# Feed-forward of a hybrid decoder layer: both products done one after the other, the second as seven products of block sums whose weight sums are made in DRAM

## The chip, the cores and the metric

The kernel runs on one core of one Trainium2 chip. The metric is device time in microseconds (us) of one launch. TensorE is called PE below, its weight loads PEld, VectorE DVE, ScalarE ACT, GpSimd POOL; SyncE is called SP and here only issues DMAs.

## The reference, cut to what matters

One layer on 512 tokens of width 2048, all in float32. A mixer (spatial gating, short convolution, gated DeltaNet) is followed by this feed-forward, a gated per-layer embedding and a last norm:

```python
h = h + concat([ya, yb, yc]) @ w_o                       # 2048 x 2048
hn = rmsnorm(h, norm_ffn)
h = h + square(relu(hn @ w_ff1)) @ w_ff2                 # 2048 -> 8192 -> 2048
hn = rmsnorm(h, norm_ple)
h = h + (p_i @ w_ple_proj) * sigmoid(hn @ w_ple_gate)
return rmsnorm(h, norm_final)
```

## The kernel before

Every float32 operand of a large product is split into a high part (a cast to fp32r, on ACT) and a low part (operand minus high part, on DVE). A product is then three matmuls, high x high, high x low and low x high (`mm3`, or the three matmul lines of `up_group`). Weights are never kept: `wload` takes a piece from DRAM into a ring `wraw` of 2816 columns (DMA on SP's queue), casts it into the ring `wh` (line 178) and subtracts into the ring `wl` (line 179). `wload` runs at a raised priority, `ahead[0]` = 200 instructions ahead of its place. Within an engine the order of instructions is fixed when the program is built, by a list scheduler; on the chip each engine runs its stream in that order.

The stages in order: input norm and first columns of `w_in`; eight DeltaNet heads (pieces of 512 columns, 16 pieces a head, the recurrence of each head mixed in by `tick`, with round trips through DRAM on SP's queue and small operations on POOL); four short convolutions; `w_o` in two halves; the feed-forward; the embedding gate and the output.

The feed-forward's first product (`up_group`) is already done as seven products instead of eight. A group `g` makes 256 hidden features for 512 tokens. For each of the 8 pairs of 128-row blocks of the input width, a 128x512 piece of `w_ff1` (four 128x128 blocks) is loaded, `pair_combos` (lines 887 to 889, DVE) adds three combinations, the whole 128x896 piece is split, and 7 x 3 matmuls of 256 columns follow. The matching combinations of the activations were made once by `fast_tiles`. At the end of a group some additions on DVE (lines 918 to 923) put the seven results together, then relu, square and a split leave the hidden features in SBUF, in one of three slots of `hidden`.

The second product (`down`) is plain. Of 16 chunks of 512 hidden features, each is multiplied with four 512-column pieces of `w_ff2` (`wload` of 128x1024), 48 matmuls of 512 columns each, and added into the residual rows `hs` in SBUF by DVE (`accumulate`, line 780). The loop at the end of the quoted text interleaves the two: one `up_group` pair of blocks, then half a `down`, so that both products run through the whole feed-forward. The up product takes the four PSUM banks `pd`, the down product the four banks `pg`. There are 32 groups, 5,376 matmuls of 256 columns, and 16 x 4 pieces, 3,072 matmuls of 512 columns.

Of the kernel before, what the change touches and what calls it, by code (L numbers as in the profile page):

```python
# [10 lines left out]
F32 = mybir.dt.float32  # L11
# [8 lines left out]
P = 128  # L20
S = 512
# [34 lines left out]
def hybrid_block(ctx: ExitStack, tc: tile.TileContext, x, p, norm_mix, w_in, sg_ln_g, sg_ln_b, sg_w,  # L56
# [102 lines left out]
    def wload(shape, parts, dst=None, combine=None):  # L159
        n = int(np.prod(shape))  # L160
        at = place(n)

        def view(t):
            t = t[:, at:at + n]
            if len(shape) == 1:
                return t
            if len(shape) == 2:
                return t.rearrange("q (a b) -> q a b", a=shape[0])
            return t.rearrange("q (a b c) -> q a b c", a=shape[0], b=shape[1])
        rv = view(ring[0])  # L170
        if dst is None:
            dst = view(ring[1]), view(ring[2])
        with tc.high_priority(offset=ahead[0]):
            for sel, src in parts:
                nc.sync.dma_start(sel(rv), src)
            if combine:
                combine(rv)
            nc.scalar.copy(dst[0], rv)  # L178
            nc.vector.tensor_tensor(dst[1], rv, dst[0].bitcast(F32), ALU.subtract)  # L179
        return dst  # L180

    def seg_parts(wdram, segs, k0, kc):
# [318 lines left out]
    if True:  # L501
# [180 lines left out]

        done = [False] * H
        gd = None
        for h in range(H):
            c = {"h": h}
            ps = [pd.tile([P, S], F32, name="d") for _ in range(2)]
            if h == 0:
                drain()
                later(sgu())  # L690
            feature_major(col_blocks(w_in, [QKV0 + 1024 + h * P, QKV0 + h * P]), 2, KD, KC2, ps)
            if h == 0:
                drain()
# [12 lines left out]
            gate_z(c, ps[1])  # L706
# [141 lines left out]
    for part in (1, 0):  # L848
        for c in range(4):
            ps, pool, nm = banks()  # L850
            token_major(w_o[part * 1024:(part + 1) * 1024], [(c * 512, 512)], lambda k: mix(8 * part + k)[0],
                        lambda k: mix(8 * part + k)[1], 8, ps, KC3)
            if part and c == 0:
                drain()
            if part:
                for tt in range(NT):
                    accumulate(tt, c, ps[tt])
                if c == 3:
                    xb = [r2b.tile([P, 16, HS], F32R, name="r2") for _ in range(2)]
# [22 lines left out]
            yield  # L882

    ss2 = res.tile([P, NT, 4], F32, name="ss2")
    def pair_combos(v):
        b = v.rearrange("q (a b) -> q a b", b=P)
        nc.vector.tensor_tensor(b[:, 4:6], b[:, 0:4:3], b[:, 1:2].broadcast_to([P, 2, P]), ALU.subtract)  # L887
        nc.vector.tensor_tensor(b[:, 1], b[:, 3], b[:, 4], ALU.add)
        nc.vector.tensor_tensor(b[:, 6], b[:, 2], b[:, 1], ALU.subtract)

    def up_group(g, pool, nm):
        ba, bb, bc_, bd = (pool.tile([P, 2, HS], F32, name=nm) for _ in range(4))

        def src(j):
            return w_ff1[2 * j * P:(2 * j + 2) * P, g * 256:(g + 1) * 256].rearrange("(a q) c -> q a c", q=P)
        for i, j in enumerate(PAIRS):
            wh, wl = wload((7 * P,), [(lambda v: v[:, :4 * P].rearrange("q (a c) -> q a c", a=2), src(j))],
                           combine=pair_combos)
            k = 2 * j
            e = list(zip(*([t[:, q] for t in z for q in range(t.shape[1])] for z in extra[j])))  # L900
            xs = [(XH[:, k, :HS], XL[:, k, :HS]), (XH[:, k + 1, :HS], XL[:, k + 1, :HS]), e[2],
                  (XH[:, k + 1, HS:], XL[:, k + 1, HS:]), e[0], e[1], (XH[:, k, HS:], XL[:, k, HS:])]
            for m, (slot, dst, half) in enumerate(((0, bc_, 0), (2, ba, 0), (3, bd, 0), (6, ba, 1), (4, bc_, 1),
                                                   (1, bb, 0), (5, bb, 1))):
                ws = slice(slot * P, (slot + 1) * P)
# [24 lines left out]
        yield  # L930

    NCH = DFF // 512
    hidden = [(t[:, o:o + 4].rearrange("q (a b) c -> q a (b c)", a=2), t[:, o + 4:o + 8].rearrange("q (a b) c -> q a (b c)", a=2))
              for t, o in ((hb[0], 0), (hb[0], 8), (hb[1], 0))]

    def up():
        for g in range(2 * NCH):
            yield from up_group(g, *((pg, "g") if g == 1 else (pd, "d")))

    def down(ch, c):  # L940
        ps, pool, nm = banks() if ch == NCH - 1 else ([pg.tile([P, 512], F32, name="g") for _ in range(NT)], pg, "g")
        for half in range(2):
            hh, hl = hidden[(2 * ch + half) % 3]
            k0 = 4 * ch + 2 * half
            wh, wl = wload((2, 512), seg_parts(w_ff2, [(c * 512, 512)], k0, 2))
            for a in range(2):
                for tt in range(NT):
                    ts = slice(tt * P, (tt + 1) * P)
                    mm3(ps[tt], hh[:, a, ts], hl[:, a, ts], wh[:, a], wl[:, a], not half and a == 0, half == 1 and a == 1)
                    tick()  # L950
            if half and ch < NCH - 1:
                for tt in range(NT):
                    accumulate(tt, c, ps[tt], rf)
            yield
        if ch == NCH - 1:
            residual(c, ps, pool, nm, ss2, KD, rf)
# [19 lines left out]
    for c in range(4):
        for _ in down(NCH - 1, c):
            pass
        if c == 1:
            pk = r2b.tile([P, 8, S], F32R, name="r2")  # L980
            pH, pL = pk[:, 0:2], pk[:, 2:4]
            entry = bg.pop()
            later(chain(entry[0], load_p(pd, "d")), entry[1])
# [86 lines left out]
```

## Time and profile before

| what | value |
|---|---|
| median of 3 runs | 2475.78 us (2475.64 to 2476.18) |
| span of the profiled execution | 2472.7 us |
| median less that span | 3.1 us |
| busy: PE, DVE, ACT, POOL | 2453.9, 1534.0, 949.1, 150.7 us |
| granted clock, mean | 0.999 |
| DMA moved | 257.30 MB, 104 GB/s over the span |

The span runs from the first to the last instruction; what is left of a run's time lies before and after it. For the profiled execution no other time than its span is listed. Busy PE counts time from a matmul's start to its modelled end, and matmuls overlap, so the pace of PE is read from the starts of neighbouring matmuls. DMA share is the mean busy share of the core's 16 DMA engines.

### The profile page before, as it was taken

How to read it: one execution, taken by the hardware profiler on the slowest of the kernel's cores; microseconds unless marked ns; L12 is line 12 of the kernel's file. 1: busy time of each engine (PE TensorE's matmuls, PEld its weight loads, DVE VectorE, ACT ScalarE, POOL GpSimd, SP SyncE). 2: the span in 40 equal slices, each digit the busy share in tenths (PEclk: the TensorE clock that was granted, in tenths of full speed). 3: DMA queues.
4: the chain of work that ended last, by engine and by line, in shares of the span. 5: the costliest groups of instructions: out<-in, count | busy, mean ns of one | idle time of the engine just before them, and what ended most of it. 6: DMA issues, size and time to landing. Idle time of an engine off the chain costs nothing.

```text
span 2472.7 us, 36948 instructions
## 1 busy us (share of the span) xinstructions
PE 2453.9 (99%) x14236; PEld 2161.9 (87%) x14236; DVE 1534.0 (62%) x2704; ACT 949.1 (38%) x1587; POOL 150.7 (6%) x325
## 2 busy tenths in 40 slices
PE   9999999999999999999999999999999999999998
PEld 8988888888888888899999999999999999987888
DVE  6754555544553477767676777767676767665334
ACT  5433333333432354333333333333333333345333
POOL 1422222222000000000000000000000000000000
PEclk9999999999999999999999999999999999999999
DMA  6433333332334223333333333333333333332233
GB/s 216 118 92 100 94 95 92 91 89 78 110 110 162 94 69 107 102 101 95 103 100 103 103 103 103 102 99 102 99 94 103 103 103 103 103 109 95 100 102 116
DMA packets 264997, 257.30 MB, mean 104 GB/s; under 512 B 29626, under 2 KB 209651, under 8 KB 263923
## 3 DMA queue, kind: packets, MB, share of 16 engines
q1 hardware_dynamic: 261796, 248.38, 32.8%
q10 hardware_dynamic: 3024, 6.55, 0.8%
q8 instruction: 112, 1.84, 0.3%
q14 instruction: 65, 0.53, 0.1%
HBM read 242.00 MB, written 12.86 MB: 103 GB/s over the span
## 4 chain that ended last, share of the span: by engine, by line
PE 92%; DVE 1%; DMA 1%; ACT 0%; issue 0%; POOL 0%; POOLq 0%; ACTq 0%
PE g L219 12%; PE g L220 12%; PE g L218 12%; PE d L911 8%; PE d L909 8%; PE d L910 8%; PE d L266 6%; PE d L268 6%; PE d L267 6%; PE d L218 2%; PE d L220 2%; PE d L219 2%; PE g L511 1%; PE g L611 1%; DMA wraw<-in_w_ff_dram 1%; PE g L618 1%
## 5 line engine op out<-in xcount | busy, mean ns | idle before, releaser
L178 ACT CAST wh<-wraw 128x896 fp32r<-128x896 f32 (+4 forms) x704 | 577.0, 821 | 1152.6 <-PE g L220 529.9
L179 DVE TENSOR_TENSOR wl<-wraw,wh 128x896 fp32r<-128x896 f32 (+4 forms) x704 | 668.0, 950 | 558.1 <-ACT wh L178 528.1
L218 PE MATMUL g<-wh,r 128*128 128x512 f32 x1128 | 440.6, 391 | 1.3 <-ACT r L224 1.2
L219 PE MATMUL g<-wl,r 128*128 128x512 f32 x1128 | 441.6, 391 | 0.2 <-DVE wl L179 0.2
L220 PE MATMUL g<-wh,r 128*128 128x512 f32 x1128 | 441.3, 392 | 0.0
L266 PE MATMUL d<-XH,wh 128*128 128x512 f32 x704 | 293.5, 417 | 0.0
L911 PE MATMUL d<-XL,wh 128*128 128x256 f32 x992 | 279.7, 282 | 0.7 <-DVE XL L228 0.7
L910 PE MATMUL d<-XH,wl 128*128 128x256 f32 x992 | 278.4, 281 | 0.7 <-DVE wl L179 0.7
L909 PE MATMUL d<-XH,wh 128*128 128x256 f32 x992 | 278.3, 281 | 0.0
L268 PE MATMUL d<-XL,wh 128*128 128x512 f32 x704 | 275.8, 392 | 0.0
L267 PE MATMUL d<-XH,wl 128*128 128x512 f32 x704 | 275.5, 391 | 0.0
L220 PEld LDWEIGHTS g<-wh,r 128*128 128x128 f32 x1128 | 211.7, 188 | 45.1
L218 PEld LDWEIGHTS g<-wh,r 128*128 128x128 f32 x1128 | 211.9, 188 | 43.6 <-ACT r L224 2.2
L219 PEld LDWEIGHTS g<-wl,r 128*128 128x128 f32 x1128 | 211.8, 188 | 42.3 <-DVE wl L179 0.5
L910 PEld LDWEIGHTS d<-XH,wl 128*128 128x128 f32 x992 | 187.2, 189 | 5.7 <-DVE wl L179 0.9
L909 PEld LDWEIGHTS d<-XH,wh 128*128 128x128 f32 x992 | 187.7, 189 | 5.1 <-issue 0.3
L911 PEld LDWEIGHTS d<-XL,wh 128*128 128x128 f32 x992 | 187.3, 189 | 1.1 <-DVE XL L228 1.1
L887 DVE TENSOR_TENSOR wraw<-wraw 128x256 f32<-128x256 f32 x256 | 108.0, 422 | 125.7 <-DMA wraw<-in_w_ff_dram 124.9
L910 PE MATMUL d<-r,wl 128*128 128x256 f32 x651 | 184.1, 283 | 0.0
L909 PE MATMUL d<-r,wh 128*128 128x256 f32 x651 | 183.7, 282 | 0.0
L780 DVE SCALAR_TENSOR_TENSOR h<-g,rf,h 128x512 f32<-128x512 f32 x248 | 178.9, 744 | 2.3 <-PE g L220 2.3
L911 PE MATMUL d<-r,wh 128*128 128x256 f32 x589 | 165.5, 281 | 0.0
(343 smaller groups left out, 3754.4 us busy)
## 6 DMA issues: line engine op xcount, KB each, us to landing
wraw<-in_w_ff_dram SPq DMA_DIRECT2D x256, 256.0 KB, 2.7
wraw<-in_w_ff_dram SPq DMA_DIRECT2D x128, 512.0 KB, 3.7
wraw<-in_w_in_dram SPq DMA_DIRECT2D x352, 128.0 KB, 2.3
wraw<-in_w_o_dram SPq DMA_DIRECT2D x64, 256.0 KB, 2.9
wraw<-in_w_ple_gate_dram SPq DMA_DIRECT2D x64, 256.0 KB, 2.9
h<-in_x_dram ACTq DMA_DIRECT2D x4, 1024.0 KB, 7.9
wraw<-in_w_in_dram SPq DMA_DIRECT2D x16, 196.0 KB, 2.6
x<-in_x_dram SPq DMA_DIRECT2D x3, 1024.0 KB, 7.3
```

The lines of the kernel that those rows point to most:

```text
L178: nc.scalar.copy(dst[0], rv)
L179: nc.vector.tensor_tensor(dst[1], rv, dst[0].bitcast(F32), ALU.subtract)
L218: nc.tensor.matmul(ps, ah, bh, start=start, stop=False)
L219: nc.tensor.matmul(ps, ah, bl, start=False, stop=False)
L220: nc.tensor.matmul(ps, al, bh, start=False, stop=stop)
L266: nc.tensor.matmul(ps, wh[:, a, b], XH[:, k], start=k == 0, stop=False)
L267: nc.tensor.matmul(ps, wl[:, a, b], XH[:, k], start=False, stop=False)
L268: nc.tensor.matmul(ps, wh[:, a, b], XL[:, k], start=False, stop=k == nk - 1)
L780: nc.vector.scalar_tensor_tensor(hc, ps, scale[:, tt:tt + 1], hc, ALU.mult, ALU.add)
L909: nc.tensor.matmul(ps, wh[:, ws], xh, start=i == 0 and m in (0, 1, 2, 5), stop=False)
L910: nc.tensor.matmul(ps, wl[:, ws], xh, start=False, stop=False)
L911: nc.tensor.matmul(ps, wh[:, ws], xl, start=False, stop=stop)
```

## The change

The two products are done one after the other.

- Groups 0 and 1 run as before. Then the residual rows `hs` (4 MB) are stored to DRAM, and their SBUF space becomes buffers for pieces of twice the size: three raw pieces and two each of high and low part, of 128x1792 (two pairs of blocks). Groups 2 to 31 use these (`up_weights`), alternately with the banks `pd` and `pg`.
- At the end of a group the hidden features are not split. Seven 128x256 tiles (four blocks and three sums) are made by three more DVE operations and written to DRAM by POOL's DMA (`hd`, 0.92 MB a group in rows of 1 KB).
- The second product views tokens as two halves, output columns as two halves of 1024, and hidden features as 32 pairs of 128-row blocks. It is done as seven products (`product`), each over the 32 pairs, each with 12 matmuls of 512 columns a pair: 2,688 matmuls. Each of the four tiles in PSUM is added into `hs` and into a scratch array after the product. Three products read `w_ff2` itself, four read sums of its blocks, `qd[0]` to `qd[3]`, 16 MB each, from DRAM. For each pair 128x1024 weights (0.5 MB) are loaded and split, for each four pairs 128x1024 activations.
- The sums `qd` are made by `presum`: 64 DMAs of 1 MB on SP's queue that copy a block from DRAM to DRAM, and 64 DMAs of 1 MB on POOL's queue that add another block onto it. `count`, called at each `wload`, issues one of these 128 steps for every 4 loads, from the first DeltaNet head on, and for every 3 loads from group 2 on (a piece of two pairs counts 2). In each round four copies are followed by four additions to copies of earlier rounds. 32 loads were counted before the first head, so 8 copies are issued there together.
- The residual rows are loaded again (4 MB) before the second product. The transposes for the gate are put behind product 6 and its end.

```diff
+NG = DFF // 256
+NST = NG // 2
+FW = D // 2
...
             nc.vector.tensor_tensor(dst[1], rv, dst[0].bitcast(F32), ALU.subtract)
+        count()
         return dst
...
+    qd = [[dram.tile([P, 2, FW + 16], F32, name=f"q{i}_{st}")[:, :, :FW] for st in range(NST)] for i in range(4)]
+    w2v = w_ff2.rearrange("(st b a q) c -> st a q b c", b=2, a=2, q=P)
+
+    def w2block(st, a, f):
+        return w2v[st, a][:, :, f * FW:(f + 1) * FW]
+
+    def presum():
+        for i in range(NST + 3):
+            if i < NST:
+                for q, a, f in ((0, 0, 0), (2, 1, 1), (3, 1, 0), (1, 1, 1)):
+                    tc.keep_in_program_order(nc.sync.dma_start(qd[q][i], w2block(i, a, f)))
+                    yield
+            for q, lag in ((0, 1), (2, 1), (1, 2), (3, 3)):
+                st = i - lag
+                if 0 <= st < NST:
+                    other = w2block(st, 0, 1) if lag == 1 else qd[0 if q == 1 else 1][st]
+                    tc.keep_in_program_order(nc.gpsimd.dma_start(qd[q][st], other, accum_op=ALU.add))
+                    yield
+
+    sums = presum()
+    pace = [0, 0]
+
+    def count(n=1):
+        pace[0] += n
+        while pace[1] and pace[0] >= pace[1]:
+            pace[0] -= pace[1]
+            next(sums, None)
...
+        pace[1] = 4
         for h in range(H):
...
     def pair_combos(v):
-        b = v.rearrange("q (a b) -> q a b", b=P)
-        nc.vector.tensor_tensor(b[:, 4:6], b[:, 0:4:3], b[:, 1:2].broadcast_to([P, 2, P]), ALU.subtract)
-        nc.vector.tensor_tensor(b[:, 1], b[:, 3], b[:, 4], ALU.add)
-        nc.vector.tensor_tensor(b[:, 6], b[:, 2], b[:, 1], ALU.subtract)
+        b = v.rearrange("q (j a b) -> q j a b", b=P, a=7)
+        n = b.shape[1]
+        for j in range(n):
+            nc.vector.tensor_tensor(b[:, j, 4:6], b[:, j, 0:4:3], b[:, j, 1:2].broadcast_to([P, 2, P]), ALU.subtract)
+        nc.vector.tensor_tensor(b[:, :, 1], b[:, :, 3], b[:, :, 4], ALU.add)
+        nc.vector.tensor_tensor(b[:, :, 6], b[:, :, 2], b[:, :, 1], ALU.subtract)
+
+    wide = []
+
+    def up_weights(g, i):
...
+        rv, wh, wl = (t[n % len(t)] for t in wide)
+        with tc.high_priority(offset=ahead[0]):
+            for j in range(2):
+                nc.sync.dma_start(rv[:, j * 7 * P:j * 7 * P + 4 * P].rearrange("q (a c) -> q a c", a=2), src(i + j))
+            pair_combos(rv)
+            nc.scalar.copy(wh, rv)
+            nc.vector.tensor_tensor(wl, rv, wh.bitcast(F32), ALU.subtract)
+        count(2)
+        return wh, wl
...
-        hh, hl = hidden[g % 3]
-        for o, t in ((0, sa), (1, v)):
-            nc.scalar.activation(t, t, AF.Relu)
-            nc.scalar.activation(t, t, AF.Square)
-            dh, dl = (z[:, o].rearrange("q (a b) -> q a b", a=2) for z in (hh, hl))
-            split(dh, dl, t)
...
+        nc.scalar.activation(s[:, :4], s[:, :4], AF.Relu)
+        nc.scalar.activation(s[:, :4], s[:, :4], AF.Square)
+        nc.vector.tensor_tensor(s[:, 4:6], s[:, 0:4:3], s[:, 2:3].broadcast_to([P, 2, HS]), ALU.subtract)
+        nc.vector.tensor_tensor(s[:, 6], s[:, 0], s[:, 5], ALU.add)
+        nc.vector.tensor_tensor(s[:, 2], s[:, 6], s[:, 1], ALU.subtract)
+        nc.gpsimd.dma_start(hd[g // 4][:, :, g % 4].rearrange("m q c -> q m c"), s)
+
+    up_group(0, pd, "d")
+    up_group(1, pg, "g")
     spot[0] = 0
     drain()
...
+    for tt in range(NT):
+        nc.sync.dma_start(hsd[tt], hs[tt])
+    hctx.close()
+    wp = hctx.enter_context(tc.tile_pool(name="wp", bufs=1))
...
+    pace[1] = 3
+    for g in range(2, NG):
+        up_group(g, *((pd, "d"), (pg, "g"))[g % 2])
+    for _ in sums:
         pass
+    hctx.close()
...
+    for tt in range(NT):
+        nc.sync.dma_start(hs[tt], hsd[tt])
...
+    def product(m, slot, wsrc):
+        pool, nm = ((pd, "d"), (pg, "g"))[m % 2]
+        ps = [[pool.tile([P, 512], F32, name=nm) for _ in range(2)] for _ in range(2)]
+        for kp in range(NG):
+            n = m * NG + kp
+            rv, wh, wl = wslots[n % len(wslots)]
+            with tc.high_priority(offset=ahead[0]):
+                if kp % 4 == 0:
...
+                    nc.sync.dma_start(xr_, hd[kp // 4][slot])
+                    split(xh, xl, xr_)
+                nc.sync.dma_start(rv, wsrc(kp))
+                split(wh, wl, rv)
+            for t in range(2):
+                ts = slice(t * P, (t + 1) * P)
+                for f in range(2):
+                    fs = slice(f * 512, (f + 1) * 512)
+                    mm3(ps[t][f], xh[:, kp % 4, ts], xl[:, kp % 4, ts], wh[:, fs], wl[:, fs], kp == 0, kp == NG - 1)
+                tick()
+        return ps
...
+    ps = product(3, 4, q2(2))
+    for t, f in PAIR4:
+        nc.vector.tensor_tensor(u(t, f), u(t, f), ps[t][f], ALU.add)
+        add(2 + t, f, u(t, f))
+        add(2 + t, 2 + f, ps[t][f], -1)
+        square(2 + t, 2 + f, ps[t][f])
...
```

There are four places `wslots` for the weights of `product`: two in the old rings, two in the space that held activation combinations of the up product (`xr`, `xb`).

## Rows read from the trace of the kernel before

**Rows 1.** The page: busy time by engine; chain that ended last, by engine.

```profile
PE 2453.9 (99%) x14236; PEld 2161.9 (87%) x14236; DVE 1534.0 (62%) x2704; ACT 949.1 (38%) x1587; POOL 150.7 (6%) x325
...
PE 92%; DVE 1%; DMA 1%; ACT 0%; issue 0%; POOL 0%; POOLq 0%; ACTq 0%
```

**Rows 2.** Windows of 62 us (`w_o`, feed-forward): busy, clock, DMA share, GB/s.

```profile
744.00:806.00 62.00, 62.00 (x268) 50.28 (x267) 23.03 (x35) 13.65 (x22) 0.00 (x0) 1.00 0.45 161
...
1488.00:1550.00 62.00, 62.00 (x392) 56.12 (x391) 45.15 (x80) 24.62 (x32) 0.00 (x0) 1.00 0.31 98
```

**Rows 3.** Timeline of PE in the feed-forward; first number the start.

```profile
1499.78 0.39 PE L218 MATMUL g<-wh,r 128*128 128x512 f32 x1
...
1503.64 0.39 PE L220 MATMUL g<-wh,r 128*128 128x512 f32 x1
1503.87 0.28 PE L909 MATMUL d<-XH,wh 128*128 128x256 f32 x1
...
1505.89 0.28 PE L911 MATMUL d<-r,wh 128*128 128x256 f32 x1
```

**Rows 4.** Groups by line and form: count, busy us, mean ns, idle before.

```profile
L179 DVE TENSOR_TENSOR wl<-wraw,wh 128x896 fp32r<-128x896 f32 x256 | 279.0, 1090 | 177.2 <-ACT wh L178 174.5
...
L178 ACT CAST wh<-wraw 128x896 fp32r<-128x896 f32 x256 | 241.2, 943 | 293.0 <-PE d L911 261.1 <-DVE wl L179 13.7 <-DVE wraw L889 9.5
...
L780 DVE SCALAR_TENSOR_TENSOR h<-g,rf,h 128x512 f32<-128x512 f32 x248 | 178.9, 744 | 2.3 <-PE g L220 2.3
...
L179 DVE TENSOR_TENSOR wl<-wraw,wh 128x1024 fp32r<-128x1024 f32 x128 | 156.1, 1220 | 55.5 <-ACT wh L178 55.5
L178 ACT CAST wh<-wraw 128x1024 fp32r<-128x1024 f32 x128 | 134.0, 1047 | 412.5 <-PE g L220 386.2 <-DVE wraw L887 13.2 <-DVE h L780 9.1
...
L887 DVE TENSOR_TENSOR wraw<-wraw 128x256 f32<-128x256 f32 x256 | 108.0, 422 | 125.7 <-DMA wraw<-in_w_ff_dram 124.9
...
L921 DVE TENSOR_TENSOR xs<-xs,d 128x512 f32<-128x512 f32 x31 | 21.1, 680 | 0.0
```

**Rows 5.** Timeline of DVE in the feed-forward.

```profile
1501.22 0.42 DVE L887 TENSOR_TENSOR wraw<-wraw 128x256 f32<-128x256 f32 x1
...
1503.33 0.42 DVE L887 TENSOR_TENSOR wraw<-wraw 128x256 f32<-128x256 f32 x1 [0.37 <-DMA wraw<-in_w_ff_dram]
...
1507.84 1.08 DVE L179 TENSOR_TENSOR wl<-wraw,wh 128x896 fp32r<-128x896 f32 x1
1510.02 1.09 DVE L179 TENSOR_TENSOR wl<-wraw,wh 128x896 fp32r<-128x896 f32 x1 [1.09 <-ACT wh L178]
```

**Rows 6.** Windows in up groups 0 and 1 (alone on PE).

```profile
930.00:940.00 10.00, 9.13 (x77) 8.93 (x77) 9.73 (x23) 4.24 (x6) 0.00 (x0) 1.00 0.34 107
```

**Rows 7.** The page, DMA issues: size, median us to landing.

```profile
wraw<-in_w_ff_dram SPq DMA_DIRECT2D x128, 512.0 KB, 3.7
...
wraw<-in_w_o_dram SPq DMA_DIRECT2D x64, 256.0 KB, 2.9
```

**Rows 8.** DMA queues at 744 to 748 us: packets, MB, share of time.

```profile
q10 hardware_dynamic: 149, 1.09, 67.6%
q1 hardware_dynamic: 143, 0.26, 30.2%
...
wraw<-in_w_o_dram SPq DMA_DIRECT2D x1, 256.0 KB, 6.9
```

**Rows 9.** Window of 744 to 758 us, `x` and `w_o` loaded together.

```profile
744.00:758.00 14.00, 14.00 (x62) 11.34 (x61) 5.41 (x9) 3.10 (x5) 0.00 (x0) 1.00 0.98 363
```

**Rows 10.** Timeline of SP in a DeltaNet head.

```profile
407.46 0.37 SPq L603 DMA_DIRECT2D T<-td  x1
```

**Rows 11.** Timeline of PE where that head's `T` is first read.

```profile
430.52 0.60 PE L511 MATMUL g<-ident,T 128*128 128x128 f32 x4
```

**Rows 12.** Timeline of POOL: the same step of two neighbouring heads.

```profile
330.85 1.01 POOL L146 TENSOR_TENSOR krs<-rs_ms,mhalf 128x4 f32<-128x4 f32 x1 [28.34 <-DVE rs_ms L145]
...
389.16 1.01 POOL L146 TENSOR_TENSOR krs<-rs_ms,mhalf 128x4 f32<-128x4 f32 x1 [28.34 <-DVE rs_ms L145]
```

More of the change, by code (lines that the diff above doesn't have):

```diff
@@ L748, in hybrid_block @@
     hs = []
+    hctx = ctx.enter_context(ExitStack())
+    hsd = dram.tile([NT, P, D], F32, name="hsd")
     def load_residual():
@@ new lines, in hybrid_block, with src @@
+    wide = []
+    def up_weights(g, i):
+        def src(j):
+            return w_ff1[2 * j * P:(2 * j + 2) * P, g * 256:(g + 1) * 256].rearrange("(a q) c -> q a c", q=P)
+        if not wide:
+            return wload((7 * P,), [(lambda v: v[:, :4 * P].rearrange("q (a c) -> q a c", a=2), src(i))],
+                         combine=pair_combos)
+        n = up_at[0]
+        up_at[0] += 1
+        rv, wh, wl = (t[n % len(t)] for t in wide)
[7 more added lines that the diff above has]
+        return wh, wl
@@ L891, in up_group @@
+    up_at = [0]
     def up_group(g, pool, nm):
         ba, bb, bc_, bd = (pool.tile([P, 2, HS], F32, name=nm) for _ in range(4))
[L894 to L900, printed above, removed]
+        per = 2 if wide else 1
+        for i in PAIRS:
+            if i % per == 0:
+                wh, wl = up_weights(g, i)
+            w0 = (i % per) * 7 * P
+            k = 2 * i
+            e = list(zip(*([t[:, q] for t in z for q in range(t.shape[1])] for z in extra[i])))
@@ L936, in up @@
[L936 to L956, printed above, removed]
@@ new lines, in hybrid_block @@
+    NW = 14 * P
+    wide.extend([[ring[0][:, :NW]] + [wp.tile([P, NW], F32, name=f"wp{i}") for i in range(2)],
+                 [ring[1][:, :NW], wp.tile([P, NW], F32R, name="wph")],
+                 [ring[2][:, :NW], wp.tile([P, NW], F32R, name="wpl")]])
+    pace[1] = 3
+    for g in range(2, NG):
+        up_group(g, *((pd, "d"), (pg, "g"))[g % 2])
+    for _ in sums:
+        pass
+    hctx.close()
+    hp = hctx.enter_context(tc.tile_pool(name="hp2", bufs=1))
+    hs[:] = [hp.tile([P, D], F32, name=f"h{tt}") for tt in range(NT)]
@@ new lines, in hybrid_block @@
+    for tt in range(NT):
+        nc.sync.dma_start(hs[tt], hsd[tt])
+    nrf = res.tile([P, NT], F32, name="nrf")
+    nc.vector.tensor_scalar(nrf, rf, -1.0, None, ALU.mult)
+    wx = r2b.tile([P, 4, FW], F32R, name="r2")
+    xw = res.tile([P, NXR, HS], F32, name="xr").rearrange("q (a b) c -> q a (b c)", a=2)
+    cuts = [slice(NW, NW + FW), slice(0, FW)]
+    wslots = [(ring[0][:, c], ring[1][:, c], ring[2][:, c]) for c in cuts] + \
+             [(xw[:, i], wx[:, i], wx[:, 2 + i]) for i in range(2)]
@@ new lines, in hybrid_block, with b2, q2 @@
+    xs0 = res.tile([P, 4, HS], F32, name="xs")
+    xslots = [s7t[:, 4 * i:4 * i + 4] for i in range(4)]
+    uscr = r1.tile([P, 8, 512], F32, name="XH")
+    def b2(a, f):
+        return lambda kp: w_ff2[(2 * kp + a) * P:(2 * kp + a + 1) * P, f * FW:(f + 1) * FW]
+    def q2(i):
+        return lambda kp: qd[i][kp // 2][:, kp % 2]
+    def product(m, slot, wsrc):
[6 more added lines that the diff above has]
+                if kp % 4 == 0:
+                    xr_ = xs0 if n == 0 else xslots[(n // 4 - 1) % 4]
+                    o = 8 * ((n // 4) % 2)
+                    xh, xl = hb[:, o:o + 4], hb[:, o + 4:o + 8]
+                    nc.sync.dma_start(xr_, hd[kp // 4][slot])
[9 more added lines that the diff above has]
+        return ps
@@ new lines, in add, with square, u, tmp @@
+    def add(tt, c, src, sign=1):
+        hc = hs[tt][:, c * 512:(c + 1) * 512]
+        sc_ = (rf if sign > 0 else nrf)[:, tt:tt + 1]
+        nc.vector.scalar_tensor_tensor(hc, src, sc_, hc, ALU.mult, ALU.add)
+    def square(tt, c, junk):
+        nc.scalar.activation(junk, hs[tt][:, c * 512:(c + 1) * 512], AF.Square, accum_out=ss2[:, tt, c:c + 1])
+    PAIR4 = [(t, f) for t in range(2) for f in range(2)]
+    def u(t, f):
+        return uscr[:, 2 * t + f]
+    def tmp(t, f):
+        return uscr[:, 4 + 2 * t + f]
@@ new lines, in hybrid_block @@
+    ps = product(0, 0, b2(0, 0))
+    for t, f in PAIR4:
+        nc.scalar.copy(u(t, f), ps[t][f])
+        add(t, f, ps[t][f])
+    ps = product(1, 6, q2(1))
+    for t, f in PAIR4:
+        nc.vector.tensor_tensor(u(t, f), u(t, f), ps[t][f], ALU.subtract)
+    ps = product(2, 5, q2(0))
+    for t, f in PAIR4:
+        nc.vector.tensor_tensor(tmp(t, f), u(t, f), ps[t][f], ALU.add)
+        add(t, 2 + f, tmp(t, f), -1)
+        add(2 + t, 2 + f, tmp(t, f), -1)
+    ps = product(3, 4, q2(2))
+    for t, f in PAIR4:
+        nc.vector.tensor_tensor(u(t, f), u(t, f), ps[t][f], ALU.add)
+        add(2 + t, f, u(t, f))
+        add(2 + t, 2 + f, ps[t][f], -1)
+        square(2 + t, 2 + f, ps[t][f])
@@ L974, in hybrid_block @@
+    ps = product(4, 1, b2(1, 0))
+    for t, f in PAIR4:
+        add(t, f, ps[t][f])
+        square(t, f, ps[t][f])
+    ps = product(5, 3, q2(3))
+    for t, f in PAIR4:
+        add(2 + t, f, ps[t][f])
+        square(2 + t, f, ps[t][f])
     XH = r1.tile([P, KD, S], F32R, name="XH")
     XL = r1.tile([P, KD, S], F32R, name="XL")
[L976 to L983, printed above, removed]
+    pk = r2b.tile([P, 8, S], F32R, name="r2")
@@ L985, in hybrid_block, with tiles @@
+    pH, pL = pk[:, 0:2], pk[:, 2:4]
+    def tiles(k0, k1, pool, nm):
+        for k in range(k0, k1):
+            plain_tile(k, pool, nm, KD)
+            yield
+    later(chain(tiles(0, KD // 2, pg, "g"), load_p(pg, "g")))
+    ps = product(6, 2, b2(1, 1))
+    drain()
+    for t, f in PAIR4:
+        add(t, 2 + f, ps[t][f], -1)
+        square(t, 2 + f, ps[t][f])
+    later(tiles(KD // 2, KD, pd, "d"))
+    sets[0] = 1
+    spot[0] = FW
     rp = res.tile([P, NT], F32, name="rp")
```

33 lines of the change are left out of this document (8 added, 25 removed).

## The prediction

> **What bounds the kernel now.** I read the page first: PE is busy 99% of the span and makes up 92% of the chain that ended last [rows 1]. So the time is a count of matmuls times their pace, as long as nothing else becomes late. The windows give the same picture by stage: PE has no gap in `w_o` or in the feed-forward, where DVE is busy 45 of 62 us, ACT 25, and the DMA engines 0.31 of the time [rows 2]. The timeline gives the pace, start to start. Eighteen matmuls of 512 columns start from 1499.78 to 1503.64, so 3.86 / 17 = 0.227 us each; eighteen of 256 columns from 1503.87 to 1505.89, 0.119 us each [rows 3]. An up group of 168 matmuls is then 19.96 us of PE, a piece of two pairs 4.99. Then I looked for what may become late: prices on DVE and ACT [rows 4, 5], the one place where the up product runs alone [rows 6], and DMA under load [rows 7 to 9].
>
> **The change, part by part.** The sum is made against the profiled execution: span 2472.7 us, and the runs shown have a median of 2475.8, 3.1 more, which I take as unchanged.
>
> *Matmuls.* The second product falls from 3,072 to 2,688 matmuls of 512 columns. 384 x 0.2272 = **-87.3 us**, on the path, since PE is the path. The up product keeps its 5,376. If the seven products ran at the pace of `w_o` (62 / 268 = 0.231 us [rows 2]) they would cost 2,688 x 0.004 = 11 us more. I take the feed-forward's pace, for the same operands.
>
> *DVE and ACT in the second product.* 248 `accumulate` of 744 ns vanish from DVE [rows 4]: 185 us, hidden behind PE now, worth 0. In their place a pair needs one split of 1024 columns and a quarter of another: DVE 1.25 x 1.22 = 1.53 us, ACT 1.25 x 1.05 = 1.31, under 12 x 0.227 = 2.73 us of PE. The additions after a product (up to twelve of 744 ns, 9 us) lie beside the next product's 87 us. 0; if that cover is gone, 9 us a product. DMA in this stage is 0.52 + 0.13 MB per 2.73 us, 240 GB/s, where 363 GB/s at a share of 0.98 was reached [rows 9]. 0.
>
> *DVE in groups 2 to 31.* From 896 to 1024 columns a split grows by 130 ns and a cast by 104 [rows 4]; so 1792 columns take 1.09 + 7 x 0.13 = 2.00 us and 0.94 + 7 x 0.104 = 1.67 us. The combinations of a piece are four operations of 256 elements, 4 x 0.42 = 1.69 us. DVE needs 3.69 us of a piece's 4.99. A group's end needs five operations of 256 and three of 512, 5 x 0.42 + 3 x 0.68 = 4.15 us. Together 4 x 3.69 + 4.15 = 18.9 of 19.96 us, 95%. In before, where the up product ran alone, DVE was busy 9.73 of 10 us and PE got 77 matmuls where 84 would fit [rows 6]; that stretch also held `fast_tiles`. With a little less work than that I take half a us a group, 30 x 0.5 = **+15 us** (0 to 60, the upper end being most of the loss in that stretch, 8%, on each group, rounded up).
>
> *DMA in groups 2 to 24.* By group 2 the counter has given (32 + 128 + 32 + 64 + 16) / 4 = 68 of the 128 steps; the other 60 take 90 pieces, 22.5 groups, so a group carries 1.33 copies and 1.33 additions of 1.05 MB. Weights of the stage move at 98 GB/s for a share of 0.31, 316 GB/s when full [rows 2]; bulk rows at 363 / 0.98 = 370 [rows 9]. Per group: weights 2.10 / 316 = 6.6 us, hidden features 0.92 / 316 = 2.9, copies 1.33 x 2.83 = 3.8; 13.3 of 19.96 us. An accumulating DMA has no row. Below, it is a copy, 2.83 us, and the engines are 86% full. It reads two streams, so the nearest end above is two copies, 5.7 us: 20.9 us a group, 0.9 too much, 20 us in all. I take half of that, **+10 us**.
>
> *Steps in the earlier stages.* Steps there come every four loads. In a head one step takes 58.31 / 16 x 4 = 14.6 us [rows 12], against 5.7 of DMA at most; `T` is read 23 us after its load is issued [rows 10, 11], so DeltaNet's trips through DRAM have cover. 0 (to 10). The eight copies in one go at the first head are 8.4 MB, 22.7 us ahead of the weights on SP's queue. The ring has five places of 512 columns, so four pieces are ahead, 4 x 3.64 = 14.6 us. What is left is 8; I take **+6 us** (0 to 8).
>
> *POOL.* What a DMA costs POOL itself has no row. Below: SP's issue, 0.37 us [rows 10]. Above: POOL's 1.01 us operation [rows 12] for every 128 rows of a DMA, 7 + 2.7 of them a group, 10 us of 20. Both are hidden; POOL has nothing else there. In the heads, 1 to 2 us more before `krs`, which DVE waits for; covered by the four pieces ahead.
>
> *First turn.* The store of `hs` is 4.19 MB, 11.3 us on SP's queue ahead of the narrow weights, with two pieces, 5 us, ahead; and the first wide cast and split, 3.7 us, need rings that the last narrow pieces still hold. Up to 10; I take **+6**. *Second turn.* Two of the four weight places are freed by the last up matmul. Loading both (2 x 1.4 us after a landing time of 3.7 less 1.4 [rows 7]), cast and split take 7.4 us against two pairs at hand, 5.5. Behind them the 4.19 MB of `hs` stand before the weights of pairs 6 and 7, some 4 us late. **+5** (2 to 14). *End.* The last additions precede half of the gate's transposes, **+3** (0 to 6).
>
> Sum: -87.3 + 15 + 10 + 6 + 6 + 5 + 3 = -42, 2475.8 - 42 = **2433 us**.
>
> **The rivals.** *All hidden.* DVE and DMA both keep up in the up stage, and only the turns, the first head and the end cost some 12 us: 2475.8 - 87.3 + 12 = 2400 us. For it: DVE's neighbouring operations overlap a little, so 95% is an upper figure. Against it: the stretch where DVE was at 97% lost PE time.
>
> *DVE in a chain.* If DVE does combinations, waits for the cast, and splits, a piece takes 1.69 + 1.67 + 2.00 = 5.36 us instead of 4.99, and with its end a group takes 25.6 us, 5.6 too many. For it: with only two wide places for `wh`, casts wait for PE, and before, the splits of 896 waited 174.5 us for ACT [rows 4]. Against it: the order is not so strict; combinations of two pieces at 1501 and 1503 stand ahead of both splits, at 1508 and 1510 [rows 5]. If half of the waits stay unfilled it is 30 x 2.8 = 84 us in place of my 15: 2502 us, and 58 us of such waits use up the gain.
>
> *Additions in DRAM dearer than two copies* (the side of slower). The engines fill up and weights starve. What else I charge is 20 us, so 67 us of gain remain for the stage, 3.0 us in each of 22.5 groups: an addition may take (6.65 + 3.0) / 1.33 = 7.2 us of all engines, 2.5 copies. At three copies, 8.5 us, a group is 24.6 us, 4.7 too many, 105 in all: 2514 us. Speaking for it: nothing spaces the additions of a group on POOL, and where bulk rows stood in another queue, the two queues had nearly equal packets, 149 and 143, though 1.09 MB against 0.26, and a `w_o` load landed after 6.9 us instead of 2.9 [rows 7, 8]. Up weights have rows of 1 KB, the sums of 4 KB; turn by turn 1 KB comes per 0.05 + 0.18 us on each engine, 71 GB/s of the 105 wanted, and 40 if an addition is two copies. Against it: PE didn't lose anything in that stretch [rows 9], and a third raw place holds a piece ahead. The Trainium skill (DMA: Bandwidth & Descriptors, Queues, rings and completion order) says that each engine goes round the queue rows with work, one packet at a time; these rows agree.
>
> **How the numbers follow.** My case 0.5, with 2412 to 2460 of its own; all hidden 0.2; DVE in a chain 0.14; dear additions 0.16. The range for 8 in 10 goes from 2399 to 2506: it takes in all hidden and a half chain, and leaves out a part of the dear additions. No change is what lies within 0.2%, 5 us, about what can be measured. Faster are the first two and a third of the chain, 0.75; same 0.04; slower 0.21.
>
> **What would show it.** In the profile after, 14236 - 384 matmuls; starts 0.227 us apart in the second product, DVE there near 55% busy, DMA near 0.65. In groups 2 to 31, 20 to 21 us a group, DVE above 90%; PE's waits there name the split (DVE) or, through it, DMA. DMA share 0.8 to 1 up to about group 24, then lower, with groups shorter after it if DMA was the limit. Gaps of PE of 5 to 10 us at the first head and at both turns. I am wrong if an addition takes over 7 us of the engines, if splits wait for casts on every piece, or if POOL's own work on a DMA is many times 1 us.

## The result, and the profile after

The changed kernel takes 2763.47 us (median of 4 runs, 2762.7 to 2765.44) where the kernel before takes 2475.71 (4 runs). The ratio is 1.1163, 95% interval 1.1147 to 1.1178: 288 us slower, against a forecast of 43 us faster. Its profiled execution has a span of 2763.7 us.

The page after: busy time by engine, and the chain that ended last, by engine.

```profile
PE 2468.5 (89%) x13852; PEld 2168.0 (78%) x13852; DVE 1520.7 (55%) x2317; ACT 1046.5 (38%) x1495; POOL 248.7 (9%) x421
...
PE 31%; DMA 17%; DVE 9%; ACT 1%; issue 0%; POOLq 0%; SPq 0%; ACTq 0%
```

The 384 matmuls are gone (13,852), yet PE is busy 14.6 us longer and idle 295 us, where it was idle 19 [rows 1]. Windows say where: heads and short convolution, one window of the up groups, and the second product.

```profile
186.00:744.00 558.00, 502.69 (x2628) 424.20 (x2626) 241.91 (x479) 179.25 (x445) 118.34 (x275) 0.95 0.62 151
...
1178.00:1240.00 62.00, 44.53 (x327) 43.72 (x326) 34.58 (x57) 18.39 (x14) 5.04 (x5) 0.87 0.76 216
...
2046.00:2542.00 496.00, 496.00 (x2177) 404.75 (x2176) 296.52 (x268) 242.41 (x256) 0.00 (x0) 1.00 0.73 233
```

The second product does what was forecast: no gap, DVE 60%. The loss is in the up stage, where PE issues 327 of the 521 matmuls that 62 us hold at 0.119 us [rows 3] and DVE is busy 56%, not 95%. A smaller loss, 55 us of idle PE, lies in stages to which the change only adds DMAs.

Waits of the up stage (us in total, times, longest): DVE's first combination (L927) waits for the load of its piece, PE for the split (L947).

```profile
DVE wp L927 <- DMA wp<-in_w_ff_dram: 240.9, 76, 10.7
...
DVE wraw L927 <- DMA wraw<-in_w_ff_dram: 106.0, 36, 10.2
...
PE d L971 <- DVE wl L947: 79.7, 16, 8.9
```

One such wait, in the timeline of all engines:

```profile
1188.44 2.02 DVE L947 TENSOR_TENSOR wpl<-wp,wph 128x1792 fp32r<-128x1792 f32 x1
1189.03 1.69 ACT L946 CAST wh<-wp 128x1792 fp32r<-128x1792 f32 x1 [3.25 <-PE d L972]
...
1190.49 0.99 SPq L944 DMA_DIRECT2D wp<-in_w_ff_dram  x2
...
1202.37 0.43 DVE L927 TENSOR_TENSOR wp<-wp 128x256 f32<-128x256 f32 x1 [10.66 <-DMA wp<-in_w_ff_dram]
1202.71 2.02 DVE L947 TENSOR_TENSOR wl<-wp,wh 128x1792 fp32r<-128x1792 f32 x1
...
1204.76 0.88 SPq L944 DMA_DIRECT2D wp<-in_w_ff_dram  x2
```

This is the whole loop. A split ends at 1190.46 and frees a raw place; its load is issued at 1190.49. The cast of the next piece ends at 1190.72, so its split could start. But DVE works in order, and the first combination of the piece still being loaded stands ahead of that split. DVE stands still for 10.66 us, the split ends at 1204.73, and the next load goes out at 1204.76. So a piece costs its landing time plus 0.4 us of combination plus 2.0 of split, 14.3 us here, against PE's 4.99. PE waited from 1195.8 to 1204.79.

Beside that load ran `hd` and three additions, issued by POOL from 1186.61 on; behind it in SP's queue stood one copy, issued at 1191.52. DMA queues from 1188 to 1203 us, POOL's first, then SP's (packets, MB, share of 16 engines):

```profile
q0 software_dynamic: 749, 2.93, 92.0%
q1 hardware_dynamic: 381, 0.37, 9.3%
```

In the earlier stages the largest single loss starts in POOL's timeline. Its `ors` waits 54 us (55 in the kernel before), and six additions that were counted out over that time leave POOL together behind it:

```profile
694.06 1.03 POOL L149 TENSOR_TENSOR ors<-rs_ms,mhalf 128x4 f32<-128x4 f32 x1 [54.23 <-DMA wraw<-in_w_in_dram]
695.07 2.14 POOL L212 DMA_DIRECT2D q<-in_w_ff_dram  x2
696.24 2.79 POOL L212 DMA_DIRECT2D q<-q  x2
697.36 3.80 POOL L212 DMA_DIRECT2D q<-in_w_ff_dram  x2
```

(A row joins issues that overlap; two more additions follow at 704.63 and 715.87.) Beside them `mix`, on its way through DRAM, comes late. ACT stands still for it, the cast of a narrow weight load stands behind that on ACT, and PE waits 24.5 us for that cast:

```profile
749.46 1.23 ACT L256 CAST r<-xs 128x512 fp32r<-128x512 f32 x2 [29.80 <-DMA xs<-mix]
...
751.47 0.79 PE L298 MATMUL d<-XH,wh 128*128 128x512 f32 x1 [24.51 <-ACT wh L181]
```

Of the 55 us, 35 are lost in the heads (186 to 682 us), where additions leave POOL two at a time. One wait there has the pattern of the loop on another engine: ACT, in order, waits with a cast for its weights, and the copy `vw`, for which PE waited 8.7 us, stands behind that cast:

```profile
255.70 0.62 ACT L181 CAST wh<-wraw 128x512 fp32r<-128x512 f32 x1 [10.57 <-DMA wraw<-in_w_in_dram]
256.23 0.26 ACT L676 COPY vw<-g 128x128 f32<-128x128 f32 x1
```

### The profile page after: what moved, and what is told of

It reads as the page before. It is cut to its first block, busy times and chain, and to the rows that moved or that the text cites. A ratio compares the mean times of both kernels' runs of the same rounds, so it can differ in the third digit from the quotient of the medians.

```text
span 2763.7 us, 35996 instructions
## 1 busy us (share of the span) xinstructions
PE 2468.5 (89%) x13852; PEld 2168.0 (78%) x13852; DVE 1520.7 (55%) x2317; ACT 1046.5 (38%) x1495; POOL 248.7 (9%) x421
## 4 chain that ended last, share of the span: by engine, by line
PE 31%; DMA 17%; DVE 9%; ACT 1%; issue 0%; POOLq 0%; SPq 0%; ACTq 0%
DMA wp<-in_w_ff_dram 11%; DMA wraw<-in_w_ff_dram 5%; PE g L252 5%; PE g L250 5%; PE g L251 5%; PE d L252 4%; PE d L251 4%; PE d L250 4%; DVE wpl L947 3%; DVE wl L947 3%; DVE wp L927 1%; DVE wraw L927 1%; DMA hd<-r 1%; PE g L971 1%; PE g L972 0%; PE g L970 0%
## 5 line engine op out<-in xcount | busy, mean ns | idle before, releaser
L182 DVE TENSOR_TENSOR wl<-wraw,wh 128x512 fp32r<-128x512 f32 (+3 forms) x336 | 250.2, 749 | 368.3 <-ACT wh L181 347.6
L181 ACT CAST wh<-wraw 128x512 fp32r<-128x512 f32 (+3 forms) x336 | 216.3, 646 | 523.6 <-PE d L300 176.4
L927 DVE TENSOR_TENSOR wp<-wp 128x256 f32<-128x256 f32 x160 | 67.4, 422 | 241.5 <-DMA wp<-in_w_ff_dram 240.9
L257 DVE TENSOR_TENSOR wl<-wraw,wh 128x1024 fp32r<-128x1024 f32 x112 | 137.2, 1225 | 102.1 <-ACT wh L256 102.1
L257 DVE TENSOR_TENSOR r<-xr,r 128x1024 fp32r<-128x1024 f32 x112 | 136.7, 1221 | 75.1 <-ACT r L256 75.1
L256 ACT CAST wh<-wraw 128x1024 fp32r<-128x1024 f32 x112 | 117.7, 1051 | 137.6 <-PE d L252 73.5
L250 PE MATMUL d<-wh,r 128*128 128x512 f32 x408 | 161.6, 396 | 2.5 <-ACT wh L181 2.0
L252 PE MATMUL d<-wh,r 128*128 128x512 f32 x408 | 160.0, 392 | 0.5 <-DVE r L257 0.5
L251 PE MATMUL d<-wl,r 128*128 128x512 f32 x408 | 160.1, 392 | 0.0
L971 PE MATMUL d<-XH,wl 128*128 128x256 f32 x272 | 86.4, 318 | 80.4 <-DVE wl L947 79.7
L250 PE MATMUL g<-wh,r 128*128 128x512 f32 x328 | 128.6, 392 | 0.0
L251 PE MATMUL g<-wl,r 128*128 128x512 f32 x328 | 128.2, 391 | 0.0
L252 PE MATMUL g<-wh,r 128*128 128x512 f32 x328 | 128.2, 391 | 0.0
```

The source lines that it names most:

```text
L250: nc.tensor.matmul(ps, ah, bh, start=start, stop=False)
L251: nc.tensor.matmul(ps, ah, bl, start=False, stop=False)
L252: nc.tensor.matmul(ps, al, bh, start=False, stop=stop)
L256: nc.scalar.copy(dh, src)
L257: nc.vector.tensor_tensor(dl, src, dh.bitcast(F32), ALU.subtract)
L971: nc.tensor.matmul(ps, wl[:, ws], xh, start=False, stop=False)
```

## The experiments

Line numbers in rows are those of each kernel. Where one profiled run stands alone, its single time is given.

**1 to 4: which transfers.** These start from the changed kernel. `e1_no_sums` makes no sums (the four products read plain blocks of `w_ff2`), `e2_copies_only` leaves out the additions, `e3_adds_as_copies` makes them plain copies on the same queue, and `e4_copies_on_act` moves the copies to ACT's queue.

```diff
 e1_no_sums
-    sums = presum()
+    sums = iter(())
-        return lambda kp: qd[i][kp // 2][:, kp % 2]
+        return b2(*((0, 0), (1, 1), (1, 1), (1, 0))[i])
 e2_copies_only
-                    tc.keep_in_program_order(nc.gpsimd.dma_start(qd[q][st], other, accum_op=ALU.add))
 e3_adds_as_copies
-                    tc.keep_in_program_order(nc.gpsimd.dma_start(qd[q][st], other, accum_op=ALU.add))
+                    tc.keep_in_program_order(nc.gpsimd.dma_start(qd[q][st], other))
 e4_copies_on_act
-                    tc.keep_in_program_order(nc.sync.dma_start(qd[q][i], w2block(i, a, f)))
+                    tc.keep_in_program_order(nc.scalar.dma_start(qd[q][i], w2block(i, a, f)))
```

> No copies and no additions in DRAM; the four products that read sums read one block of w_ff2 instead (so the output is not the reference's), all else as in the changed kernel. Theory A (loads of up weights come late because copies and additions share the DMA engines with them) and rival B (only the copies, ahead in SP's own queue) both expect the loss to vanish: the profile after shows 21.6 us a group once the sums are done, so 30 groups take 648 us, the products 615, the rest as before: 2410 to 2450 us. Rival C (the up product alone on PE, with wide pieces, is what costs): above 2600 us.

> The 64 copies stay, the 64 additions are left out (so the sums are not sums). In the profile after a group took 25 us with no addition behind its hidden features, 28 with one and 37 with three. Theory A: additions cost some 4 us each in the up stage, 130 us, and about half of the early stages' loss: 2580 to 2640 us. Rival B: 2700 us or more, nearly nothing gained. If the additions are everything: below 2480 us.

> The 64 additions become plain copies of the same blocks on the same queue of POOL (the sums are not sums). It tells the second stream that an addition reads from the sharing of the engines. If an addition hurts by its longer turns on an engine: half of the additions' part goes, 2680 to 2710 us. If it hurts only by being there, turn by turn: 2750 us or more. If its price is all in the addition: 2600 to 2640 us, as without additions.

> The 64 copies are issued on ACT's queue instead of SP's, so that no weight load stands behind a copy in its own queue. Rival B: 2640 to 2690 us, the copies' part of the loss gone. Theory A (the engines are shared turn by turn, whatever the queue): 2740 to 2800 us.

Measured, with the kernel before at 2474.5 us: 2468.15, 2501.45, 2645.07 and 2768.35. Added in this order, the copies cost 33 us, a second stream of plain copies in POOL's queue 144 more, and making these additions 118 more. Copies in ACT's queue change nothing, so it is not their place ahead of the weights in SP's queue. `e2_copies_only` and `e3_adds_as_copies` lie outside every range set for them. The surprise is `e1_no_sums`, also above its 2410 to 2450: with no sums at all, 6 us of the 87 are left. A wait row and a window of the up groups of `e1_no_sums` show why:

```profile
DVE wp L927 <- DMA wp<-in_w_ff_dram: 96.3, 60, 4.1
...
1116.00:1488.00 372.00, 348.64 (x2806) 338.92 (x2805) 293.32 (x471) 154.70 (x118) 15.10 (x16) 0.99 0.42 135
```

The DMA engines are at 0.42 and loads land in 3.7 us, but DVE still waits for them: the same loop, 3.7 + 0.4 + 2.0, is over 4.99 us. PE gets 2,806 matmuls where 3,139 fit.

**5 and 6: the order alone.** The first combination of a wide piece is tied behind the split of the piece two before (`LAG = 1`); no engine gets more or less work.

```diff
-            nc.vector.tensor_tensor(b[:, j, 4:6], b[:, j, 0:4:3], b[:, j, 1:2].broadcast_to([P, 2, P]), ALU.subtract)
+            ins = nc.vector.tensor_tensor(b[:, j, 4:6], b[:, j, 0:4:3], b[:, j, 1:2].broadcast_to([P, 2, P]), ALU.subtract)
+            if behind is not None:
+                tc.add_manual_dep(ins.ins, behind.ins.name, mybir.DependencyInfo(
+                    mybir.DependencyClass.NoSync, mybir.DependencyReason.DATA), reason="order")
...
+            pair_combos(rv, behind=splits[-1 - LAG] if len(splits) > LAG else None)
...
+            splits.append(nc.vector.tensor_tensor(wl, rv, wh.bitcast(F32), ALU.subtract))
```

> No sums in DRAM (four products read blocks of w_ff2, as in e1), and DVE's order in the up stage is pinned: the combinations of a wide piece stand behind the split of the piece two before. Theory A (the order closes a loop: a raw place comes free with a split, its next load lands, and DVE, in order, waits with its first combination for that load ahead of the next split): the loop now spans two pieces, (landing 3.6 + combinations 1.69 + split 2.0) / 2 = 3.6 us a piece, under PE's 4.99, so groups of 20 to 20.5 us instead of 22.4 and about 2405 to 2420 us. Theory B (DVE's 95% load, or splits that wait for casts, is what costs): groups stay at 22.4 us and the time at 2465.

> The whole change with the same pin of DVE's order. Theory A: at a landing of about 8 us beside the sums a piece costs (8 + 1.69 + 2.0) / 2 = 5.85 us, 23.4 us a group instead of 30, so about 2580 to 2600 us; the loss of the stages before the feed-forward, some 65 us, stays. Theory C (the accumulating DMAs use up the engines, so that no order helps): it stays at 2740 to 2765.

Without sums 2400.38 us, 68 less than `e1_no_sums`, by an order on DVE. The same window, and DVE's timeline, now split first:

```profile
1116.00:1488.00 372.00, 371.96 (x3139) 371.57 (x3138) 325.05 (x523) 171.76 (x131) 16.95 (x18) 1.00 0.49 153
```

```profile
1303.15 2.02 DVE L953 TENSOR_TENSOR wpl<-wraw,wph 128x1792 fp32r<-128x1792 f32 x1
1305.09 0.75 DVE L930 TENSOR_TENSOR wp<-wp 128x256 f32<-128x256 f32 x2
...
1307.74 2.02 DVE L953 TENSOR_TENSOR wl<-wp,wh 128x1792 fp32r<-128x1792 f32 x1 [0.30 <-ACT wh L952]
1309.69 0.75 DVE L930 TENSOR_TENSOR wraw<-wraw 128x256 f32<-128x256 f32 x2
```

DVE is busy 87% and PE has no gap, so DVE's load costs nothing. With sums the pin gives 78 us, 2685.35: the direction of theory A, but under half of the size that it gave. By its own formula, (landing + 3.7) / 2 is under 4.99 only up to a landing of 6.3 us, and in `e6_order` loads into `wp` took 7.0 us in the median and up to 20.5 (1116 to 1488 us); whether that is all of the shortfall was not worked out.

**7 and 8: loads further ahead.** Five load places of 128x1024 with the combinations in tiles of their own, instead of three of 128x1792; `e8_deep` also takes a step of the sums every four up loads, not three.

```diff
-                 nc.sync.dma_start(rv[:, j * 7 * P:j * 7 * P + 4 * P].rearrange("q (a c) -> q a c", a=2), src(i + j))
+                nc.sync.dma_start(lt[:, j * 4 * P:(j + 1) * 4 * P].rearrange("q (a c) -> q a c", a=2), src(i + j))
...
-    wide.extend([[ring[0][:, :NW]] + [wp.tile([P, NW], F32, name=f"wp{i}") for i in range(2)],
+    wide.extend([[ring[0][:, i * FW:(i + 1) * FW] for i in range(2)] +
+                 [wp.tile([P, FW], F32, name=f"wp{i}") for i in range(3)],
+                 [ring[0][:, 2 * FW:], wp.tile([P, 6 * P], F32, name="wc")],
...
-    pace[1] = 3
+    pace[1] = 4
```

> No sums, pinned order, and five places of 1024 columns for loads, with the combinations in tiles of their own. Theory A: loads are far enough ahead that their landing is out of the loop; groups of 20 us, about 2400 to 2410 us; what is left above 2400 is the first turn. Theory B: 2465 still.

> The whole change with pinned order, five load places and a step of the sums every four loads in the up stage (instead of three). Theory A: 20.5 to 22 us a group while sums run, about 2490 to 2520 us, of which some 65 us are lost ahead of the feed-forward as before. Theory C: the groups with additions stay at 28 to 37 us and the time above 2650.

2397.31 and 2506.11 us. Without sums little is left to gain (3 us, about what runs of one kernel differ by). With them it is 179 us less than `e6_order`. A window of `e8_deep` in the up stage, and one where the six additions still leave together:

```profile
1302.00:1364.00 62.00, 62.00 (x526) 62.00 (x525) 54.45 (x100) 30.49 (x35) 7.25 (x7) 1.00 0.95 273
...
682.00:744.00 62.00, 40.46 (x175) 32.00 (x174) 13.07 (x24) 9.41 (x20) 8.89 (x9) 0.84 0.88 188
```

The DMA engines are 95% busy and PE loses nothing: theory C, that the engines' capacity is the limit, falls. The loads land no sooner than in `e6_order` (8.1 us in the median, up to 18.6, in the same stretch); what differs is how far ahead they are. The slower pace of the sums was changed in the same run; it is not told apart here, but `e10_spread_shallow` below has three places, no copies beside them, and still loses. What stays above `e7_deep_no_sums`, 109 us, is the early stages and the two turns.

**9 to 11: when the additions leave.** `e9_spread` (from `e8_deep`) and `e10_spread_shallow` (from `e6_order`) call copies and additions separately; `e11_gated` (from `e9_spread`) also makes POOL wait before an addition outside the heads, and leaves some copies for the up stage.

```diff
 e9_spread, e10_spread_shallow
             nc.sync.dma_start(diag(td[h]), tb)
+            next(adds, None)
...
             rstd(ors, cc, NT, P)
+            next(adds, None)
...
+                apace[:] = 0, 8
...
+        if g == 4:
+            pace[:], apace[:] = [0, 4], [0, 5]
 e11_gated
             nc.sync.dma_start(diag(td[h]), tb)
-            next(adds, None)
...
-        pace[1] = 4
+        pace[:] = [48, 6]
...
+            if at is not None:
+                tc.keep_in_program_order(nc.gpsimd.tensor_copy(gate, ring[2][:, at:at + 1].bitcast(F32)))
+            next(adds, None)
...
-                apace[:] = 0, 8
+                pace[:], apace[:] = [0, 5], [0, 5]
...
-            pace[:], apace[:] = [0, 4], [0, 5]
+            pace[:], apace[:] = [0, 8], [0, 5]
```

> As e8 (the whole change, pinned order, five load places), with the sums spread by hand: copies every four loads through the early stages, so that all 64 are done before the up stage; one addition behind each head's trip of T and one behind each head's last rstd, then one every eight loads up to the up stage (26 of 64); none in the first four up groups, then one every five loads. Theory D (the 65 us ahead of the feed-forward come from additions that queue up behind POOL's waiting instructions and then run two to five at once beside the narrow loads): no early loss, first turn as without sums, second turn without additions; about 2397 + 10 to 30 = 2405 to 2430 us, under the kernel before. Theory E (any addition beside the heads costs, bunched or not): at least 20 of the 65 us stay and the turns as well, 2450 to 2480 us, no better than the kernel before.

> The same spreading, with pinned order but the change's own three load places (as e6). If three places suffice once copies are out of the up stage and additions come one at a time: within 20 us of e9. If one addition at a time already makes the weights land in 8 us and more, 23 us a group as forecast for e6: some 90 us over e9, about 2500 us.

> As e9, but the additions are really spaced: behind the heads each waits on POOL for a copy of one column (128x1) of the split of a weight load, every five loads, so that none is issued before that load's time; in the heads one addition behind each head's last rstd instead of two, and a copy every six loads instead of four. Theory D (bunches cost, single additions do not): the 28 us that e9 lost from 682 to 744 and the 12 from 744 to 806 go, and most of the 3 to 6 us in each window of the heads; what is left over the 2397 us without sums is 10 to 25 us, so 2407 to 2425 us, faster than before. Theory E (any addition beside narrow loads costs): the loss spreads over the stage instead of going, 2450 to 2490 us.

`e9_spread` misses both its ranges: 2490.19 us, ratio 1.0065 (1.0048 to 1.0082). POOL's timeline tells why. Behind the last `ors` nothing in POOL's order waits for time to pass, so the eleven additions meant for the stages up to the first up group left within 35 us:

```profile
685.44 1.03 POOL L149 TENSOR_TENSOR ors<-rs_ms,mhalf 128x4 f32<-128x4 f32 x1 [54.11 <-DVE rs_ms L148]
686.45 1.85 POOL L217 DMA_DIRECT2D q<-q  x2
687.64 2.78 POOL L217 DMA_DIRECT2D q<-in_w_ff_dram  x2
688.76 2.57 POOL L217 DMA_DIRECT2D q<-q  x1
```

Each 62 us of the heads lost 2 to 6 us too. `e10_spread_shallow` takes 2711.12 us, more than `e6_order`, though no copies are left in its up stage. A window there:

```profile
1240.00:1302.00 62.00, 43.34 (x336) 42.93 (x336) 38.52 (x63) 20.22 (x15) 5.10 (x5) 0.83 0.59 149
```

Three load places do not carry even additions without copies, at 0.59 of the engines. (They still leave in ones and twos right behind `hd`, so additions one at a time were not tried with three places.) The 2500 us forecast for that case took a landing of 8 us; loads into `wp` took 10.8 in the median (1116 to 1488 us), which by the formula above is 7.3 us a piece, and DVE waited up to 9.1 us for one. Why they land later than in `e6_order` stays open.

`e11_gated` takes 2428.1 us (4 runs, 2425.98 to 2432.73), ratio 0.9812 (0.9796 to 0.9829): faster than the kernel before by 1.9%, and 335 us faster than the change. Its additions in `w_o` are 10 to 14 us apart, each behind a small copy that waits for a split:

```profile
767.57 0.18 POOL L234 COPY gate<-wl 128x1 f32<-128x1 f32 x1 [17.51 <-DVE wl L182]
767.69 1.04 POOL L217 DMA_DIRECT2D q<-in_w_ff_dram  x1
780.47 0.18 POOL L234 COPY gate<-wl 128x1 f32<-128x1 f32 x1 [11.73 <-DVE wl L182]
780.70 1.04 POOL L217 DMA_DIRECT2D q<-in_w_ff_dram  x1
```

Two windows of it, beside those of `e8_deep`:

```profile
682.00:744.00 62.00, 56.70 (x235) 45.49 (x234) 27.74 (x34) 20.18 (x31) 3.51 (x6) 0.94 0.80 218
...
1302.00:1364.00 62.00, 62.00 (x525) 62.00 (x525) 55.78 (x98) 29.47 (x35) 8.33 (x8) 1.00 0.97 264
```

The heads lose nothing. Theory D holds for the stages behind the heads: of the 29 and 12 us of idle PE that `e9_spread` has in the windows from 682 to 806 us, 5 and 0 are left. The time ends 3 us above its range, as those 5 us are still lost and 7 more from 868 to 930 us, where the narrow up groups run beside additions. `e11_gated` also has one addition less a head and fewer copies there than `e9_spread`, so the heads' part is not put down to one of the two.

## Why the prediction was wrong

**Matmuls, -87.3 us: right.** In `e7_deep_no_sums` PE is busy 2372.5 us, 81.4 less than before. Most of the difference is the pace in the second product, 271 matmuls in 62 us or 0.2288 us each in place of 0.2272; 2,688 x 0.0016 = 4 of the 6 us.

**DVE in groups 2 to 31, +15: the step that failed first.** It added up DVE's operations and asked whether they fit in a group. They do: 87%, no loss (`e5_order_no_sums`). What it did not follow is what stands behind what on DVE, and what the split at the back releases. I had the rows: two combinations ahead of both splits [rows 5]. I read them as proof that DVE does not idle for casts, where they show that a split waits behind a load. The loop cost 68 us without any sum, where I had 15, which alone uses up most of what the matmuls give. The rival "DVE in a chain" had the wrong link in it: in the wide groups (1054 to 1984 us) DVE waited 7 us in all for casts and 338 for loads.

**DMA in groups 2 to 24, +10: right price, wrong question.** This term is the larger failure: the sums cost 295 us of the change's time (`e1_no_sums`), at most 65 of them as idle PE ahead of the up stage. From the shares of POOL's queue, (0.163 x 2763.7 - 0.040 x 2395.3) / 64 = 5.5 us of all engines for an addition, where `e7_deep_no_sums` gives what `hd` takes. In `e3_adds_as_copies` a plain copy comes to (0.107 x 2643.4 - 95.8) / 64 = 2.9 us. So an addition is 1.9 copies, at my upper end and not dearer; the third rival's condition, 2.5 copies, is not met, though its sign is what came. With 5.5 us the sum of capacity gives +16, and even that is not paid: `e8_deep` and `e11_gated` run at 0.95 and 0.97 of the engines without a gap. The price is the landing time. I had the two signs of it, additions that nothing spaces and a `w_o` load at 6.9 us in place of 2.9 [rows 7, 8], and dismissed them with a third raw place that "holds a piece ahead". It holds none: its load is the one that DVE stands waiting for. The Trainium skill (DMA: Bandwidth & Descriptors, Queues, rings and completion order) has an engine go round the queues packet by packet. The rows of 1188 to 1203 us show 749 packets against 381, and from 1191 to 1202 us, when both queues had work, it is 483 against 319, not equal numbers; so they bear it out only in that a weight's short packets waited among long ones.

**Steps in the earlier stages, 0 (to 10): wrong.** 55 us of idle PE from 186 to 744 us, and 10 from 744 to 992. Copies on SP's queue alone cost nothing from 186 to 744 us (PE is busy 557.8 of 558 in `e2_copies_only`). What POOL issues does, 31 us as plain copies (`e3_adds_as_copies`) and 55 as additions: POOL keeps it behind its own waiting instructions and lets it go in bursts. I counted POOL's time for a DMA (about 1 us, within my bounds), not its order. I assumed one step per 14.6 us.

**The eight copies at the first head, +6: 0.** PE is busy 62.00 us of 62 to 124 in both kernels, but the cover of four pieces that I counted on was not put to the test. The text on the change says that eight copies are issued there together, and my 22.7 us rest on that. SP's timeline shows them one by one from 95.50 to 129.57 us, with weight loads between them:

```profile
95.50 0.67 SPq L206 DMA_DIRECT2D q<-in_w_ff_dram  x1
98.50 2.65 SPq L178 DMA_DIRECT2D wraw<-in_w_in_dram  x3
101.20 0.56 SPq L206 DMA_DIRECT2D q<-in_w_ff_dram  x1
```

**Turns, +6 and +5: about half of that without the sums.** `e7_deep_no_sums` loses 2.6 us more than before in 868 to 992 and 2.9 at the second turn (1550 to 1612). The end's +3 was not taken apart. The time of the rival "all hidden", 2400 us, came out only where the loop was gone and no sums were made; with the sums the best was 2428.

## What to carry to other kernels

When a step's work is priced, write down the engine's order too: for each wait, what stands behind it, and whether that instruction frees the very buffer whose load is waited for; if it does, the loop's time (landing + work) sets the pace, whatever the shares of engines and DMA. Background transfers cost here through the landing time of the loads beside them, so they are to be sized against how far ahead those loads are, and spaced by something that waits for time to pass, not by where they stand in a program. An engine that waits on others is a poor timer for DMAs issued from its queue.

## What had not been expected of the hardware

A long wait of PE costs again after it ends. Timeline of PE behind the wait of 8.99 us, two windows of that stretch, and ahead of them one behind a wait of 1.41 us, which ended at 1190.52:

```profile
1204.79 0.58 PE L971 MATMUL g<-XH,wl 128*128 128x256 f32 x1 [8.99 <-DVE wl L947]
...
1209.64 0.41 PE L972 MATMUL g<-XL,wh 128*128 128x256 f32 x1
...
1210.13 0.28 PE L972 MATMUL g<-XL,wh 128*128 128x256 f32 x1
1210.25 0.28 PE L970 MATMUL g<-r,wh 128*128 128x256 f32 x1
```

```profile
1190.50:1195.80 5.30, 5.28 (x42) 5.08 (x42) 1.15 (x3) 0.62 (x3) 0.11 (x1) 1.00 0.99 176
...
1204.70:1210.00 5.30, 5.21 (x24) 5.22 (x25) 1.75 (x6) 0.00 (x0) 0.00 (x0) 0.51 1.06 259
1210.00:1213.00 3.00, 2.31 (x20) 2.10 (x18) 0.99 (x2) 0.73 (x1) 0.00 (x0) 1.00 1.03 382
```

After the 8.99 us the granted clock is 0.51 (1.2 of 2.4 GHz) and matmuls start 0.21 us apart, then 0.12 again; after the 1.41 us it stayed at 1.00. Over the kernel, PE is busy 2468.5 us, at a mean granted clock of 0.947, for the same 13,852 matmuls that take 2372.5 at 0.998 in `e7_deep_no_sums`. Of the 368 us of span between these two, 96 are busy time and 272 idle, so a forecast that adds up the waits of this kernel alone is short by a third of them.
